# Index scores in blocks of four heads, logits of the first two query blocks for all eight heads, and six softmax steps at new places

## The chip, the cores and the metric

The kernel runs on one core of one Trainium2 chip. The metric is device time in microseconds: the median of three runs for the kernel before, with one profiled execution beside them whose trace is read here.

## The reference

One layer of a decoder trunk, 512 tokens of 1024 channels, batch 1. Cut to what the change touches:

```python
proj = h @ w_in                       # q_att 512, c_kv 128, q_idx 512, k_idx 64, w_idx 8, cv_b/cv_c/cv_x 512 each, two gates 1024 each
raw = einsum('bqhd,bsd->bqhs', q_idx, k_idx) * 64**-0.5       # 8 index heads of 64
score = einsum('bqhs,bqh->bqs', relu(raw), w_idx * 8**-0.5)   # summed over the heads
score = where(causal, score, -inf)
_, sel = top_k(score, 128)                                    # 128 keys for each query
logits = (q_lat . c_sel) * 64**-0.5                           # 8 heads, only the selected keys
probs = softmax(where(valid, logits, -inf));  att = probs @ values
conv_y = cv_b * causal_dwconv(cv_c * cv_x)                    # width 3
merged = sigmoid(g_att) * (att @ w_br_att) + sigmoid(g_conv) * (conv_y @ w_br_conv)
h = layer_norm(ALPHA * h + merged @ w_o);  then a gated MLP with a convolution, and a second layer_norm
```

The first query block of 128 needs no selection (128 keys or fewer are before it), so scores are computed for query blocks 1 to 3 only. "Selected" is turned into a mask: a selected key gets 0, any other a large negative number (`madd`), and the logits are computed for all keys of the causal block and masked.

## The kernel before

All products run on TensorE in split precision: a float32 operand becomes a high part (`wh`, a cast on ScalarE) and a low part (`wl`, the rest, a subtraction on VectorE or on POOL), and `mm3` multiplies high by high, high by low and low by high. A weight chunk of 128 output columns (`fm`) is 8 x 3 = 24 products of 128x128 weights by 512 tokens into one PSUM bank. The weights stream: SP issues the load of a raw chunk (`wr`), `advance` makes its two parts a few steps ahead of use.

The program is written by hand in order: a list of steps, each of which emits its instructions on every engine; each engine runs its own queue in that order. What can wait for what follows from the tiles. `ps` gives PSUM tiles from one rotation of 8 banks; a ninth tile waits until the first of the eight has been read. SBUF tiles of 512 columns (`k2`) rotate over 8 places, larger ones (`k4`) over 28.

The steps around the change, in the order of the program:

- The small projections (key latent, index key, index weights), and the first half (256 tokens) of two convolution chunks, kind c and kind x. Their two PSUM banks (`half_...`, the x chunk's is `half_246`) stay in use until the second halves are done.
- Four index query chunks (`qidx`, j = 0 to 3), each for two heads: 24 products of 384 columns, then a split (`qi0` to `qi3`). After j = 1 the index keys are transposed (`small_keys`, tile `kiT`). 
- Index scores (`scores(b, heads)`): for a query block b and two heads, `mm3_pair` makes 6 products that have only 64 rows, two heads side by side in the two halves of the array, each head in its own bank (`raw`). ScalarE takes the relu into `rl` (8 places), and VectorE adds it, times the head's weight, to the running `score` of that block. The first score block of the program (heads 0, 1 for b = 3, 2, 1) follows j = 2, the second j = 3, the third the second half of the c chunk, the fourth that of the x chunk.
- The second halves: `cvc` copies c to SBUF; `cvx` multiplies x (still in its PSUM bank) by it on VectorE (`cvu`), and `conv_mix` makes three scaled copies on ScalarE (`cvt`, `tap1`, `tap0`), which POOL adds up.
- Then the list `order`: the b chunk of the convolution (the first `cv` product), four attention query chunks (`qatt`), nine convolution chunks (j = 1 to 3), from index 14 on the gates `g` (24 products of 512 columns, 5.4 us) and branch products `r`. After index 8 comes `kproj`, after 10 `vproj`. While these run, VectorE has the selection (`topk`: 16 rounds of `max` and `match_replace` for each of the blocks 1 to 3) beside its ordinary work.
- Attention steps are put ahead of some of these chunks: `ATT_AT` gives their places relative to index 14. Step n makes the logits and the softmax (`att_a`) of one (group of four heads, query block), and transposes the probabilities of step n - 1 (`att_b`); `att_c` at the end of a group multiplies by the values.

A softmax step of four heads: logits on TensorE (`lg`, 12 products of 64 rows), mask and maximum on VectorE, exponentials on ScalarE into `p` with their sums, normalisation on VectorE (L659), and one step later 4 x (b + 1) transposes on TensorE into `pT`.

Of the kernel before, what the change touches and what calls it, by code (L numbers as in the profile page):

```python
# [8 lines left out]
F32 = mybir.dt.float32  # L9
# [4 lines left out]
P = 128  # L14
S = 512
D = 1024
NB = S // P
# [66 lines left out]
class Kern:  # L84
# [2 lines left out]
    LEAD = 3  # L87
    NK4 = 28
    SIDE_NS = 3600
    ATT_AT = (-2, 0, 2, 4, 6, 8, 9, 10, 12, 14)  # L90

    def __init__(self, ctx, tc, a, out):
        self.ctx, self.tc, self.nc, self.a, self.out = ctx, tc, tc.nc, a, out
# [65 lines left out]
    def mm3_pair(self, heads, qs, n):  # L159

        for qp, kp in ((0, 0), (0, 1), (1, 0)):
            for o, q, k, half in heads:
                rows = slice(half * 64, half * 64 + 64)
                self.nc.tensor.matmul(o, q[rows, qp, qs], k[rows, kp, :n], start=qp + kp == 0, stop=qp == 1)
        return [x[0] for x in heads]

    def rstd(self, var):

# [326 lines left out]
    def plan(self):  # L495
        nc, a = self.nc, self.a
# [18 lines left out]

        def wa(i, **kw):
            return chunk(a["w_a"][i], **kw)
# [40 lines left out]
        def scores(b, heads):  # L558
            SB = (b + 1) * P
            if b not in self.score:  # L560
                self.score[b] = self.k4(f"score{b}", F32, (P, SB))
            sc = self.score[b]
            os = self.mm3_pair([(self.ps("raw")[:, :SB], self.qiT[h // 2], self.kiT, h % 2) for h in heads],
                               slice((b - 1) * P, b * P), SB)
            for h, o in zip(heads, os):
                rl = self.k2(f"rl{b}_{h}")[:, :SB]
                nc.scalar.activation(rl, o, AF.Relu, scale=SCALE)
                prev = self.tri[:, S - SB:] if h == 0 else sc
                nc.vector.scalar_tensor_tensor(sc, rl, self.widx[b][:, h:h + 1], prev,
                                               op0=OP.mult, op1=OP.add)  # L570
# [62 lines left out]

        self.attT = []

        def att_a(g, b):
            SB = (b + 1) * P
            qs = slice(b * P, (b + 1) * P)
            mx = self.sm("mx", [P, 4], bufs=2)
            sums = self.sm("sums", [P, 4], bufs=2)  # L640
            pt = [self.k4(f"p{g}_{b}_{i}", F32, (P, 2, S)) for i in range(2)]
            os = []
            for j in (2 * g, 2 * g + 1):
                os += self.mm3_pair([(self.ps("lg")[:, :SB], self.qaT[j], self.kT[j], i) for i in range(2)], qs, SB)
            for i in range(4):
                l = pt[i // 2][:, i % 2, :SB]
                nc.vector.tensor_tensor_reduce(l, os[i], self.madd[b], 1.0, -3.0e38, OP.add, OP.max,
                                               mx[:, i:i + 1])
            nmx = self.sm("nmx", [P, 4], bufs=2)
            nc.vector.tensor_scalar(nmx, mx, -SCALE, None, op0=OP.mult)  # L650
            for i in range(4):
                l = pt[i // 2][:, i % 2, :SB]
                nc.scalar.activation(l, l, AF.Exp, bias=nmx[:, i:i + 1], scale=SCALE,
                                     accum_out=sums[:, i:i + 1])
            rs = self.sm("rs", [P, 4], bufs=2)
            nc.vector.reciprocal(rs, sums)
            for i in range(4):
                l = pt[i // 2][:, i % 2, :SB]
                nc.vector.tensor_scalar(l, l, rs[:, i:i + 1], None, op0=OP.mult)  # L659
            return pt  # L660

        def att_b(g, b, pt):
            pv = self.pv.setdefault(g, {})
            for c in range(b + 1):
                t = self.ps("pT")
                for i in range(4):
                    nc.tensor.transpose(t[:, i * P:(i + 1) * P], pt[i // 2][:, i % 2, c * P:(c + 1) * P],
                                        self.ident)
                if c == b and b % 2:
                    pv[c, b // 2] = self.k2(f"pT{g}_{b}_{c}", F32, (P, 4, P))  # L670
                elif (c, b // 2) not in pv:
                    pv[c, b // 2] = self.k4(f"pT{g}_{b}_{c}", F32, (P, 4, 2 * P))
                at = slice(0, P) if c == b else slice(b % 2 * P, b % 2 * P + P)
                nc.scalar.copy(pv[c, b // 2][:, :, at], t.rearrange("p (h t) -> p h t", h=4))

        def att_c(g):

            for j in range(2 * g, 2 * g + 2):
                o = self.ps("at")
                for half in range(2):  # L680
                    for c in range(2 * half + 2):
                        for i in range(2):
                            x = self.pv[g][c, half][:, 2 * j - 4 * g + i]
                            n = x.shape[-1]
                            h = 2 * j + i
                            nc.tensor.matmul(o[64 * i:64 * i + 64, 256 * half + 256 - n:256 * half + 256],
                                             self.vals[c][:, 64 * h:64 * h + 64], x,
                                             start=c == 0, stop=c == 2 * half + 1, skip_group_check=True)
                t = self.k4(f"at{j}", F32R, (P, 2, S))
                self.evac_split(t[:, 0], t[:, 1], o)  # L690
                self.attT.append(t)
            del self.pv[g]

        self.att_state, self.pv = {}, {}
        seq = [(g, b) for g in range(2) for b in range(NB)]

        def att_step(n):

            def f():
                if n in (5, 9):  # L700
                    att_c(n // 9)
                if 0 <= n - 1 < len(seq):
                    g, b = seq[n - 1]
                    att_b(g, b, self.att_state.pop(n - 1))
                if 0 <= n < len(seq):
                    g, b = seq[n]
                    while b not in self.ready:
                        next(self.side)
                    self.att_state[n] = att_a(g, b)
            return f  # L710


# [103 lines left out]
            return chunk(a["w_b"][i], **kw)  # L816


        def and_scores(j, fn):
            def f():  # L820
                fn()
                if j < 0:
                    self.small_keys()
                    return
                for b in (3, 2, 1):
                    scores(b, range(2 * j, 2 * j + 2))
            return f

        early = [(wa(8 + i, lo="vp"[i], resident=True), kind) for i, kind in enumerate("cx")]
# [1 line left out]
            w.second = in_halves(lambda o, kind=kind: fns[kind](o, 0), w)  # L831
        for j in range(4):
            fn = qidx(j, w := wa(j))
            step(and_scores(j - 2, fn) if j else fn, [w])
        for i, (w, kind) in enumerate(early):
            step(and_scores(2 + i, w.second), [w])
            w.need = 0


# [18 lines left out]
        order = [("b", 0)] + [("q", j) for j in range(4)] + [(kind, j) for j in range(1, 4) for kind in "cxb"]  # L858
        att_at = {len(order) + at: n for n, at in enumerate(self.ATT_AT)}
        order += [("g", 0, 0), ("g", 0, 1), ("g", 1, 0), ("g", 1, 1), ("r", 0, 1),  # L860
# [109 lines left out]
        for kk in range(4):  # L970
            w = wb(kk)
# [42 lines left out]
        pc, w = chunk(a["p_T"]), wb(9)  # L1014
# [292 lines left out]
        for j in range(NF):  # L1307
            if j in BY_BLOCKS:
                for n in range(3):
                    w = chunk(wsum[j][n - 1]) if n else wa(36 + 2 * j)  # L1310
# [5 lines left out]
            for which in (0, 1):  # L1316
                w = wa(36 + 2 * j + which)
# [26 lines left out]
        pairs = BY_BLOCKS[:EARLY], BY_BLOCKS[EARLY:]  # L1344
# [7 lines left out]
        for n, (name, i) in enumerate(copies):  # L1352
            at = at_ple - 2 + n // 2 if n < 4 else at_ple + 1 + (n - 4) * 4 // 5 if n < 20 else at_ple + 16 + 3 * (n - 20)
# [3 lines left out]
        n = len(those)  # L1357
# [317 lines left out]
```

## Time and profile before

| | |
|---|---|
| median of 3 runs | 737.0 us (736.82 to 738.28) |
| profiled execution | 736.87 us, span of the trace 735.1 us, mean granted TensorE clock 0.997 |
| TensorE | 725.5 us busy, 99% of the span, 4255 products |
| VectorE | 590.1 us, 80% |
| ScalarE | 409.9 us, 56% |
| POOL | 243.4 us, 33% |
| chain of work that ended last | TensorE 98%, VectorE 1%, ScalarE 1% |

Shares over the whole span mix stages with different limits. In the rows that follow, a timeline row gives start in us, busy us, engine, line, operation, output and inputs, size, and the number of instructions; what stands in brackets is the idle time ahead of it and what ended it. In a row of the windows view the columns behind the stretch and its length are PE, PEld (weight loads), VectorE, ScalarE, POOL, SP, each with its count, then the granted clock, the DMA share and the GB/s.

### The profile page before, as it was taken

What the parts mean: (1) busy time and instruction counts of PE and PEld (TensorE: products, weight loads), DVE (VectorE), ACT (ScalarE), POOL (GpSimd) and SP (SyncE); (2) the same over time, 40 slices, a digit from 0 to 9 for tenths busy, and PEclk for the clock granted to TensorE, in tenths of its full rate; (3) what the DMA queues carried; (4) which work ended last, traced back from release to release, by engine and by line L of the source; (5) the groups of instructions that cost most, each with busy time, mean ns of one, the idle gap of its engine ahead of it and who ended that gap; (6) DMA issues with size and microseconds to landing.
All of it is one profiled execution on the core that took longest, in us unless ns stands there. A gap on an engine that the chain in (4) does not pass through costs nothing.

```text
span 735.1 us, 11836 instructions
## 1 busy us (share of the span) xinstructions
PE 725.5 (99%) x4255; PEld 633.8 (86%) x4255; DVE 590.1 (80%) x1015; ACT 409.9 (56%) x688; POOL 243.4 (33%) x326
## 2 busy tenths in 40 slices
PE   9999999999999999999999999999999999999996
PEld 5998888888877788888888999999999998888885
DVE  5867999864545266879889899999999889978797
ACT  4647424566656415342675666777767765665640
POOL 4303575555442755010101233343422112311002
PEclk9999999999999999999999999999999999999998
DMA  9372598789997999889767998998899778999761
GB/s 350 109 286 101 159 369 295 238 276 230 190 197 151 230 195 305 302 287 357 299 260 235 301 302 228 251 246 236 247 247 237 223 222 213 277 250 256 256 198 75
DMA packets 61866, 178.00 MB, mean 242 GB/s; under 512 B 7232, under 2 KB 7360, under 8 KB 61424
## 3 DMA queue, kind: packets, MB, share of 16 engines
q1 hardware_dynamic: 43248, 138.43, 53.5%
q0 software_dynamic: 17264, 36.31, 27.6%
q10 hardware_dynamic: 1296, 2.51, 1.0%
q8 instruction: 33, 0.54, 0.3%
q14 instruction: 25, 0.20, 0.1%
HBM read 171.46 MB, written 70.78 MB: 330 GB/s over the span
## 4 chain that ended last, share of the span: by engine, by line
PE 98%; DVE 1%; ACT 1%; issue 0%; DVEq 0%; POOL 0%; POOLq 0%; ACTq 0%
PE ffb L1230 26%; PE dn L1412 5%; PE dn L1413 5%; PE dn L1411 5%; PE gt L155 4%; PE gt L157 4%; PE gt L156 4%; PE cv L155 3%; PE cv L157 2%; PE cv L156 2%; PE wo L812 2%; PE wo L811 2%; PE wo L813 2%; PE br L155 2%; PE br L156 2%; PE br L157 2%
## 5 line engine op out<-in xcount | busy, mean ns | idle before, releaser
L141 DVE TENSOR_TENSOR wl<-wr,wh 128x1024 fp32r<-128x1024 f32 (+1 forms) x171 | 195.4, 1159 | 42.0 <-ACT wh L74 41.1
L74 ACT CAST wh<-wr 128x1024 fp32r<-128x1024 f32 (+1 forms) x182 | 178.1, 986 | 78.1 <-PE dn L1413 11.0
L1338 POOL TENSOR_TENSOR behind<-token,neghalf 128x1 f32<-128x1 f32 x112 | 79.6, 846 | 276.8 <-ACT token L1337 209.7
L1230 PE MATMUL ffb<-hsl,wh 128*128 128x256 f32 x304 | 86.1, 283 | 0.0
L1230 PE MATMUL ffb<-hsh,wl 128*128 128x256 f32 x304 | 86.1, 283 | 0.0
L1230 PE MATMUL ffb<-hsh,wh 128*128 128x256 f32 x304 | 86.1, 283 | 0.0
L1230 PE MATMUL ffb<-h1T,wh 128*128 128x256 f32 x456 | 83.7, 283 | 0.0
L1230 PEld LDWEIGHTS ffb<-h1T,wh 128*128 128x128 f32 x456 | 71.3, 192 | 0.1
L1230 PE MATMUL ffb<-h1T,wl 128*128 128x256 f32 x228 | 64.6, 283 | 0.0
L1230 PEld LDWEIGHTS ffb<-hsh,wh 128*128 128x128 f32 x304 | 58.4, 192 | 0.0
L1230 PEld LDWEIGHTS ffb<-hsl,wh 128*128 128x128 f32 x304 | 58.4, 192 | 0.0
L1230 PEld LDWEIGHTS ffb<-hsh,wl 128*128 128x128 f32 x304 | 58.4, 192 | 0.0
L155 PE MATMUL gt<-hT,wh 128*128 128x512 f32 x128 | 50.5, 394 | 0.0
L156 PE MATMUL gt<-hT,wh 128*128 128x512 f32 x128 | 49.9, 390 | 0.0
L157 PE MATMUL gt<-hT,wl 128*128 128x512 f32 x128 | 49.9, 390 | 0.0
L141 POOL TENSOR_TENSOR wl<-wr,wh 128x1024 fp32r<-128x1024 f32 x15 | 36.2, 2419 | 29.3 <-ACT wh L74 29.3
L1230 PEld LDWEIGHTS ffb<-h1T,wl 128*128 128x128 f32 x228 | 43.8, 192 | 0.0
L173 POOL TENSOR_TENSOR rstd<-veps,neghalf 128x1 f32<-128x1 f32 x12 | 7.1, 591 | 101.4 <-DVE nm L196 67.8
L1203 POOL DMA_DIRECT2D ws<-ws x38 | 36.5, 1333 | 3.6 <-issue 2.2
L1203 POOL DMA_DIRECT2D ws<-in_w_a x38 | 36.0, 1361 | 3.1 <-issue 1.5
L155 PE MATMUL cv<-hT,wh 128*128 128x512 f32 x80 | 31.4, 392 | 0.0
L157 PE MATMUL cv<-hT,wl 128*128 128x512 f32 x80 | 31.2, 390 | 0.0
(336 smaller groups left out, 1929.4 us busy)
## 6 DMA issues: line engine op xcount, KB each, us to landing
wr<-in_w_a SPq DMA_DIRECT2D x61, 512.0 KB, 4.4
ws<-in_w_a SPq DMA_DIRECT2D x76, 256.0 KB, 6.0
wr<-ws SPq DMA_DIRECT2D x38, 512.0 KB, 6.1
ws<-in_w_a POOLq DMA_DIRECT2D x38, 256.0 KB, 8.1
ws<-ws POOLq DMA_DIRECT2D x38, 256.0 KB, 8.3
wr<-in_w_b SPq DMA_DIRECT2D x15, 512.0 KB, 5.6
wr<-in_w_dn SPq DMA_DIRECT2D x15, 512.0 KB, 6.6
wr<-in_w_a SPq DMA_DIRECT2D x19, 256.0 KB, 6.6
```

Source lines behind the costliest of these rows:

```text
L74: nc.scalar.copy(hi, raw)
L141: (self.nc.vector if eng == "v" else self.nc.gpsimd).tensor_tensor(lo, raw, hi.bitcast(F32), op=OP.subtract)
L155: t.matmul(out, wh, xh, start=start, stop=False)
L156: t.matmul(out, wh, xl, start=False, stop=False)
L157: t.matmul(out, wl, xh, start=False, stop=stop)
L811: nc.tensor.matmul(o, act[:, 0, tb], wh, start=start, stop=False, skip_group_check=not check)
L1203: return lambda: nc.gpsimd.dma_start(to, what, accum_op=OP.add, max_dma_last_dim=4096)
L1230: nc.tensor.matmul(o, l[:, c], r, start=start and c + i == 0, stop=stop and c == 3 and i == 2, skip_group_check=True)
L1338: nc.gpsimd.tensor_tensor(self.sm("behind", [P, 1], bufs=2), t, self.neghalf, op=OP.mult)
L1411: nc.tensor.matmul(o, ah, wh[:, i, c], start=first, stop=False, skip_group_check=free)
L1412: nc.tensor.matmul(o, ah, wl[:, i, c], start=False, stop=False, skip_group_check=free)
L1413: nc.tensor.matmul(o, al, wh[:, i, c], start=False, stop=last, skip_group_check=free)
```

## The change

Three things. Scores are made for four heads at a time, so there are two score blocks and not four: heads 0 to 3 behind index query chunk j = 3, heads 4 to 7 behind the second half of the x chunk. A new function, `pair_blocks`, makes each pair of heads by itself and puts as many results into a bank as fit (two of 256 columns, four of 128). The softmax steps of query blocks 0 and 1 take both groups of heads at once, so there are six softmax steps and not eight; their probabilities lie in smaller tiles. And `ATT_AT` has eight places in the place of ten. The new numbers put the steps at indices 12, 14, 16, 19, 21, 23, 26, 28 of `order`; they were at 12, 14, 16, 18, 20, 22, 23, 24, 26, 28.

```diff
-    ATT_AT = (-2, 0, 2, 4, 6, 8, 9, 10, 12, 14)
+    ATT_AT = (-2, 0, 2, 5, 7, 9, 12, 14)
...
+    def pair_blocks(self, nm, pairs, qs, n):
+
+        os, per = [], S // n
+        for i, (q, k) in enumerate(pairs):
+            if i % per == 0:
+                banks = [self.ps(nm) for _ in range(2)]
+            at = slice(i % per * n, i % per * n + n)
+            os += self.mm3_pair([(banks[half][:, at], q, k, half) for half in range(2)], qs, n)
+        return os
...
-            os = self.mm3_pair([(self.ps("raw")[:, :SB], self.qiT[h // 2], self.kiT, h % 2) for h in heads],
-                               slice((b - 1) * P, b * P), SB)
+            os = self.pair_blocks("raw", [(self.qiT[h // 2], self.kiT) for h in heads[::2]],
+                                  slice((b - 1) * P, b * P), SB)
...
-        def att_a(g, b):
+        def att_a(gs, b):
...
-            pt = [self.k4(f"p{g}_{b}_{i}", F32, (P, 2, S)) for i in range(2)]
-            os = []
-            for j in (2 * g, 2 * g + 1):
-                os += self.mm3_pair([(self.ps("lg")[:, :SB], self.qaT[j], self.kT[j], i) for i in range(2)], qs, SB)
+            n = 4 * len(gs)
+            mx, sums, nmx, rs = (self.sm(x, [P, 8], bufs=2)[:, :n] for x in ("mx", "sums", "nmx", "rs"))
+            ls = []
+            for g in gs:
+                if b == 0:
+                    t = self.k2(f"p{g}_{b}", F32, (P, 4, SB))
+                    ls += [t[:, i] for i in range(4)]
+                elif b == 1:
+                    t = self.k4(f"p{g}_{b}", F32, (P, 4, SB))
+                    ls += [t[:, i] for i in range(4)]
+                else:
+                    t = [self.k4(f"p{g}_{b}_{i}", F32, (P, 2, S)) for i in range(2)]
+                    ls += [t[i // 2][:, i % 2, :SB] for i in range(4)]
+            os = self.pair_blocks("lg", [(self.qaT[2 * g + i], self.kT[2 * g + i]) for g in gs for i in range(2)],
+                                  slice(b * P, (b + 1) * P), SB)
...
-        seq = [(g, b) for g in range(2) for b in range(NB)]
+        seq = [((0, 1), 0), ((0, 1), 1), ((0,), 2), ((0,), 3), ((1,), 2), ((1,), 3)]
...
-                if n in (5, 9):
-                    att_c(n // 9)
+                if n in (5, 7):
+                    att_c(n // 7)
                 if 0 <= n - 1 < len(seq):
-                    g, b = seq[n - 1]
-                    att_b(g, b, self.att_state.pop(n - 1))
+                    gs, b = seq[n - 1]
+                    ls = self.att_state.pop(n - 1)
+                    for i, g in enumerate(gs):
+                        att_b(g, b, ls[4 * i:4 * i + 4])
...
-                for b in (3, 2, 1):
-                    scores(b, range(2 * j, 2 * j + 2))
+                for b in (3, 2, 1):
+                    scores(b, range(2 * j, 2 * j + 4))
...
-            step(and_scores(j - 2, fn) if j else fn, [w])
+            step(fn if j in (0, 2) else and_keys(fn) if j == 1 else and_scores(0, fn), [w])
         for i, (w, kind) in enumerate(early):
-            step(and_scores(2 + i, w.second), [w])
+            step(and_scores(2, w.second) if i else w.second, [w])
```

The rest of `att_a` is as before, with loops over 4 or 8 heads. The order of instructions moves at three places that matter below.

TensorE, the score block behind the second half of the x chunk. `raw` is a bank with scores, `qi2` and `qi3` the index queries of heads 4, 5 and 6, 7; "waits" names the engine whose work must be done first. Before, its first and last rows and the b chunk behind it:

```order
L164 MATMUL raw_289_952<-kiT_669,qi3_788 128x512 [waits Activation_49]
L164 MATMUL raw_290_953<-kiT_669,qi3_788 128x512 [waits Activation_49]
...
L164 MATMUL raw_293_980<-kiT_669,qi3_788 128x256 [waits Activation_49]
L164 MATMUL raw_294_981<-kiT_669,qi3_788 128x256 [waits Activation_49]
...
L155 MATMUL cv_299_1018<-hT0_178,wh17_757 128x512 [waits Activation_49]
```

And after:

```order
L164 MATMUL raw_281_908<-kiT_669,qi2_709 128x512 [waits Activation_49]
...
L164 MATMUL raw_287_944<-kiT_669,qi3_743 128x384 [waits Activation_49]
L164 MATMUL raw_288_945<-kiT_669,qi3_743 128x384 [waits DVE_49]
...
L164 MATMUL raw_289_964<-kiT_669,qi2_709 128x256 [waits Activation_49]
L164 MATMUL raw_290_965<-kiT_669,qi2_709 128x256 [waits Activation_49]
...
L164 MATMUL raw_290_965<-kiT_669,qi3_743 128x256
L155 MATMUL cv_295_1014<-hT0_178,wh17_712 128x512 [waits Activation_49]
```

Six banks became ten (raw_281 to raw_290); the eighth, raw_288, waits for VectorE, the ninth and tenth for ScalarE.

VectorE, from the last score updates ahead of `cvu0` (the product that reads the x chunk's bank) on. `rl1_4` is the relu of query block 1, head 4. Before:

```order
L569 SCALAR_TENSOR_TENSOR score1_742<-rl1_4_901,widx_204_195,score1_742 128x256
L569 SCALAR_TENSOR_TENSOR score1_742<-rl1_5_904,widx_204_195,score1_742 128x256
L141 TENSOR_TENSOR wl19_908<-wr19_585,wh19_907 128x1024
L743 TENSOR_TENSOR cvu0_942<-half_246_449,cvc0_863 128x512
L569 SCALAR_TENSOR_TENSOR score3_712<-rl3_6_960,widx_206_197,score3_712 128x512
```

And after:

```order
L579 SCALAR_TENSOR_TENSOR score1_804<-rl1_2_825,widx_204_195,score1_804 128x256
L579 SCALAR_TENSOR_TENSOR score1_804<-rl1_3_828,widx_204_195,score1_804 128x256
L141 TENSOR_TENSOR wl19_864<-wr19_585,wh19_863 128x1024
L757 TENSOR_TENSOR cvu0_898<-half_246_449,cvc0_861 128x512
L579 SCALAR_TENSOR_TENSOR score3_746<-rl3_4_924,widx_206_197,score3_746 128x512
```

Before, the updates of six heads stood ahead of `cvu0` and those of two behind; now it is four and four, and all of the four ahead come from the one block behind j = 3.

ScalarE, the exponentials of the second group (`p1_...`) and the casts between them, one cast (`wh`) to a chunk of products. Before:

```order
L653 ACTIVATE p1_1_1_2467,sums_486_2465<-p1_1_1_2467,nmx_491_2488 128x256 x2
L74 CAST wh42_2500<-wr42_2168 128x1024
...
L653 ACTIVATE p1_2_1_2565,sums_503_2563<-p1_2_1_2565,nmx_508_2586 128x384 x2
L74 CAST wh43_2598<-wr43_2202 128x1024
L674 COPY pT1_2_0_2657<-pT_520_2652 128x4x128
```

And after:

```order
L668 ACTIVATE p1_2_1_2405,sums_463_2401<-p1_2_1_2405,nmx_464_2402 128x384 x2
L74 CAST wh41_2436<-wr41_2103 128x1024
L74 CAST wh42_2467<-wr42_2153 128x1024
...
L686 COPY pT1_2_0_2573<-pT_488_2568 128x4x128
```

Between the exponentials of a step and the copies of its transposed probabilities there was one chunk's cast; now there are two.

More of the change, by code (lines that the diff above doesn't have):

```diff
@@ L634, in plan @@
         self.attT = []
-        def att_a(g, b):
+        def att_a(gs, b):
             SB = (b + 1) * P
-            qs = slice(b * P, (b + 1) * P)
-            mx = self.sm("mx", [P, 4], bufs=2)
-            sums = self.sm("sums", [P, 4], bufs=2)
-            pt = [self.k4(f"p{g}_{b}_{i}", F32, (P, 2, S)) for i in range(2)]
-            os = []
-            for j in (2 * g, 2 * g + 1):
-                os += self.mm3_pair([(self.ps("lg")[:, :SB], self.qaT[j], self.kT[j], i) for i in range(2)], qs, SB)
-            for i in range(4):
-                l = pt[i // 2][:, i % 2, :SB]
+            n = 4 * len(gs)
[13 more added lines that the diff above has]
+                                  slice(b * P, (b + 1) * P), SB)
+            for i, l in enumerate(ls):
@@ L647, in att_a @@
                 nc.vector.tensor_tensor_reduce(l, os[i], self.madd[b], 1.0, -3.0e38, OP.add, OP.max,
                                                mx[:, i:i + 1])
-            nmx = self.sm("nmx", [P, 4], bufs=2)
             nc.vector.tensor_scalar(nmx, mx, -SCALE, None, op0=OP.mult)
-            for i in range(4):
-                l = pt[i // 2][:, i % 2, :SB]
+            for i, l in enumerate(ls):
                 nc.scalar.activation(l, l, AF.Exp, bias=nmx[:, i:i + 1], scale=SCALE,
                                      accum_out=sums[:, i:i + 1])
-            rs = self.sm("rs", [P, 4], bufs=2)
@@ L656, in att_a, with att_b @@
             nc.vector.reciprocal(rs, sums)
-            for i in range(4):
-                l = pt[i // 2][:, i % 2, :SB]
+            for i, l in enumerate(ls):
                 nc.vector.tensor_scalar(l, l, rs[:, i:i + 1], None, op0=OP.mult)
-            return pt
-        def att_b(g, b, pt):
+            return ls
+        def att_b(g, b, ls):
             pv = self.pv.setdefault(g, {})
@@ L666, in att_b @@
                 for i in range(4):
-                    nc.tensor.transpose(t[:, i * P:(i + 1) * P], pt[i // 2][:, i % 2, c * P:(c + 1) * P],
-                                        self.ident)
+                    nc.tensor.transpose(t[:, i * P:(i + 1) * P], ls[i][:, c * P:(c + 1) * P], self.ident)
                 if c == b and b % 2:
@@ L694, in plan @@
         self.att_state, self.pv = {}, {}
-        seq = [(g, b) for g in range(2) for b in range(NB)]
+        seq = [((0, 1), 0), ((0, 1), 1), ((0,), 2), ((0,), 3), ((1,), 2), ((1,), 3)]
         def att_step(n):
             def f():
-                if n in (5, 9):
-                    att_c(n // 9)
+                if n in (5, 7):
+                    att_c(n // 7)
                 if 0 <= n - 1 < len(seq):
-                    g, b = seq[n - 1]
-                    att_b(g, b, self.att_state.pop(n - 1))
+                    gs, b = seq[n - 1]
+                    ls = self.att_state.pop(n - 1)
+                    for i, g in enumerate(gs):
+                        att_b(g, b, ls[4 * i:4 * i + 4])
                 if 0 <= n < len(seq):
-                    g, b = seq[n]
+                    gs, b = seq[n]
                     while b not in self.ready:
                         next(self.side)
-                    self.att_state[n] = att_a(g, b)
+                    self.att_state[n] = att_a(gs, b)
             return f
@@ L816, in wb, with and_keys, f @@
             return chunk(a["w_b"][i], **kw)
+        def and_keys(fn):
+            def f():
+                fn()
+                self.small_keys()
+            return f
         def and_scores(j, fn):
@@ L821, in f @@
                 fn()
-                if j < 0:
-                    self.small_keys()
-                    return
                 for b in (3, 2, 1):
-                    scores(b, range(2 * j, 2 * j + 2))
+                    scores(b, range(2 * j, 2 * j + 4))
             return f
```

## The prediction

> **What bounds the kernel.** I read the page's span and chain, then the stages, then TensorE's waits, then the timelines of each engine where the diff works.
>
> ```profile
> span 735.1 us, 11836 instructions
> PE 98%; DVE 1%; ACT 1%; issue 0%; DVEq 0%; POOL 0%; POOLq 0%; ACTq 0%
> 67.10:137.60 70.50, 70.50 (x311) 58.40 (x312) 64.53 (x149) 31.76 (x50) 46.33 (x27) 1.00 0.72 244
> PE pT L667 <- DVE p L659: 0.6, 1, 0.6
> ```
>
> TensorE carries 98% of the chain, so a change is worth what it moves on TensorE's queue. VectorE is close behind in the stage after the index scores: 64.53 of 70.50 us. Whatever makes TensorE wait for VectorE's queue there is paid in full.
>
> **Part 1, fewer switches to 64-row products.** One such block in the old order, with its neighbours:
>
> ```profile
> 60.07 0.28 PE L156 MATMUL half<-hT,wh 128*128 128x256 f32 x1
> 60.19 0.28 PE L157 MATMUL half<-hT,wl 128*128 128x256 f32 x1
> 60.40 1.84 PE L164 MATMUL raw<-kiT,qi 64*128 64x512 f32 x18
> 62.17 0.39 PE L155 MATMUL half<-hT,wh 128*128 128x256 f32 x1
> 62.39 0.28 PE L156 MATMUL half<-hT,wh 128*128 128x256 f32 x1
> ```
>
> The half chunk's products follow each other every 0.12 us. Into the block it is 0.21 (0.09 more); the block takes 1.77 to the next product where its nine pairs at 0.23, 0.17 and 0.12 us (the spacing of products of 512, 384 and 256 columns) make 1.55 (0.22 more); the product behind it takes 0.22 (0.10 more). A switch in and out costs 0.41 us. Four score blocks become two (-0.8), eight logit blocks six (-0.8 by the same price).
>
> **Part 2, ten banks wanted by one score block, eight there.** The first new block stands right behind the fourth index query chunk.
>
> ```profile
> 49.17 1.85 PE L164 MATMUL raw<-kiT,qi 64*128 64x512 f32 x18
> 51.19 0.44 PE L155 MATMUL qi<-hT,wh 128*128 128x384 f32 x1 [0.16 <-ACT rl L567]
> 55.55 1.85 PE L164 MATMUL raw<-kiT,qi 64*128 64x512 f32 x18
> 50.54 1.09 ACT L567 ACTIVATE rl<-raw 128x512 f32<-128x512 f32 x2 [0.78 <-PE raw L164]
> 56.55 0.60 ACT L567 ACTIVATE rl<-raw 128x512 f32<-128x512 f32 x1 [0.41 <-PE raw L164]
> ```
>
> Without the block at 49.17 that chunk starts at 49.17 - 0.09 = 49.08 instead of 51.19, and its first product is not slow (0.1), so the block starts 2.2 us before 55.55, at 53.3. The old order already once waited for a relu (0.16). Relus of 512 columns come every 0.49 us, the first 1.0 us after the block's start: the fourth ends at 53.3 + 1.0 + 3 x 0.49 + 0.6 = 56.4. The built program lets the tenth bank wait for that one. Unhindered TensorE would be there at 53.3 + 2.5 = 55.8, so it stalls 0.6, and the c chunk's second half starts at 57.3, about when it did (57.34). The x chunk's follows with no block between; its 48 products end the stretch at 63.0, and the second block starts at 63.2, 2.0 us before the old fourth one.
>
> There the eighth bank (raw_288) is the one in which the x chunk was summed. It is free when VectorE has run cvu0, the product that reads it; the ninth and tenth wait for the block's first two relus, and ScalarE has those behind cvt and two taps, which also wait for cvu0. Queued ahead of cvu0 on VectorE are the first block's twelve score updates and wl19:
>
> ```profile
> 51.17 0.75 DVE L569 SCALAR_TENSOR_TENSOR score<-rl,widx,tri 128x512 f32<-128x512 f32 x1 [0.82 <-ACT rl L567]
> 52.02 0.75 DVE L569 SCALAR_TENSOR_TENSOR score<-rl,widx,score 128x512 f32<-128x512 f32 x1
> 59.96 2.67 DVE L569 SCALAR_TENSOR_TENSOR score<-rl,widx,score 128x256 f32<-128x256 f32 x1
> 63.14 3.84 DVE L569 SCALAR_TENSOR_TENSOR score<-rl,widx,score 128x512 f32<-128x512 f32 x6
> 66.89 1.22 DVE L141 TENSOR_TENSOR wl<-wr,wh 128x1024 fp32r<-128x1024 f32 x1
> 68.03 0.68 DVE L743 TENSOR_TENSOR cvu<-half,cvc 128x512 f32<-128x512 f32 x1
> 59.96 2.39 POOL L141 TENSOR_TENSOR wl<-wr,wh 128x1024 fp32r<-128x1024 f32 x1 [19.99 <-ACT wh L74]
> 67.58 1.68 POOL L607 TENSOR_TENSOR w_uk<-w_uk_raw,w_uk 128x512 fp32r<-128x512 f32 x1 [5.23 <-ACT w_uk L606]
> ```
>
> Updates begin 0.63 after the first relu's start (51.17 behind 50.54): 53.3 + 1.0 + 0.63 = 54.95. Six take 3.84; twelve take 7.7, and 0.4 more since four in a row on one score each wait 0.1 for the last write (51.17 + 0.75 to 52.02): 63.05. The update at 59.96 took 2.67 instead of some 0.5: POOL's wl18 began with it, and it ended 0.28 behind POOL. In the new order ScalarE's cast for wl18 again follows the relus, again near 58.8, so an update that begins at about 60.3 is held to 62.35 + 0.4: 1.9 more, 64.95. Then wl19 (1.22) and cvu0 from 66.0.
>
> One more POOL product can stand in the way, w_uk's low half:
>
> ```profile
> 63.25 0.34 ACTq L604 DMA_DIRECT2D w_uk_raw<-in_w_uk  x1
> 66.89 0.62 ACT L606 CAST w_uk<-w_uk_raw 128x512 fp32r<-128x512 f32 x1 [2.16 <-DMA w_uk_raw<-in_w_uk]
> 68.81 0.82 ACT L729 ACTIVATE cvt<-cvu,vec 128x512 f32<-128x512 f32 x1 [1.30 <-DVE cvu L743]
> 70.76 1.05 ACT L567 ACTIVATE rl<-raw 128x512 f32<-128x512 f32 x2
> 67.02 0.50 PE L155 MATMUL cv<-hT,wh 128*128 128x512 f32 x1
> DMA to landing us min/median/max: 2.8/2.8/2.8
> ```
>
> Its load is issued once ScalarE's queue has passed the c half's wait, near 60.5, and lands 3.6 us later (63.25 to 66.89) or 2.8 (its sister load w_uv_raw, the last line); with the cast POOL starts between 64.0 and 64.8 and runs 1.68, just where the last updates and wl19 stand. Held, VectorE loses 0.9 to 1.5. I take 1.2: the window covers wl19's start in most of its width. cvu0 then starts at 67.2. From there: in the old order the second relu behind cvu0 ended at 70.76 + 1.05 = 71.81, 3.78 after cvu0's start; then three pairs of 256 columns for the second half of that bank and three before them (0.6 to the last), 0.2 out of the block. So the b chunk (cv, 67.02 before) starts 4.6 us after cvu0, at 71.8: +4.8 for the scores, the two saved switches already in it. Bounds: cvu0 at 66.0 gives +3.6; both POOL products out of the way +1.8; no bank wait at all -1.0 (0.8 and the old 0.2 wait). Topk begins some 2 to 4 us later, TensorE more than that, so VectorE's backlog gets no nearer.
>
> **Part 3, the spacing.** In the old order the last softmax steps stood one product apart:
>
> ```profile
> 190.81 0.60 PE L667 MATMUL pT<-ident,p 128*128 128x128 f32 x4
> 191.34 0.89 PE L164 MATMUL lg<-kT,qa 64*128 64x128 f32 x12
> 214.94 1.46 PE L667 MATMUL pT<-ident,p 128*128 128x128 f32 x8
> 216.33 1.34 PE L164 MATMUL lg<-kT,qa 64*128 64x384 f32 x12
> 222.95 0.39 PE L157 MATMUL br<-cvT,wl 128*128 128x512 f32 x1
> 223.98 2.19 PE L667 MATMUL pT<-ident,p 128*128 128x128 f32 x12 [0.64 <-DVE p L659]
> 226.10 1.65 PE L164 MATMUL lg<-kT,qa 64*128 64x512 f32 x12
> ```
>
> Four undisturbed transposes take 0.53 with the switch behind them, 0.11 each. Eight should take 0.97 and took 1.39; twelve should take 1.4 and took 2.12, and stood 0.8 late (222.95 to 223.98, where 0.23 is due). With 0.1 ahead of the eight that is 2.0 us of waiting for p. Now two or three products (5.4 us each) stand between, against one. All of it goes: -2.0. With two logit blocks less -2.8.
>
> What may be late next is p of the eight-head steps.
>
> ```profile
> 156.98 1.14 DVE L659 TENSOR_SCALAR p<-p,rs 128x256 f32<-128x256 f32 x4
> 162.24 0.93 PE L667 MATMUL pT<-ident,p 128*128 128x128 f32 x7
> ```
>
> Four heads of block 1 were ready at 158.1, 4.1 us before their transposes. Eight heads cost some 1.4 (maxima), 2.0 (exponentials) and 1.1 (this row) more, 4.5, and block 0's 3.2 more stand ahead in the same queue; against it TensorE comes 4.8 (scores) and 1.8 (its own added logits and transposes) later there, less VectorE's 2 to 3.5 in the backlog. That nets to a slack of 0 to 2 us: 0.1 for the forecast, up to 1 at the upper end. Fewer small operations and the halved k4 use change nothing on TensorE's queue: VectorE works beside it.
>
> **Sum.** +4.8 - 2.8 + 0.1 = +2.1, and I shade it to +1.9 because a stall's end can fall with work already queued. The profiled execution took 736.87, 0.1 under the runs' median of 737.0, so 738.8 us. The before runs spread 736.82 to 738.28: 0.2% (1.5 us) is what a measurement can tell.
>
> **Rivals.** (a) POOL's w_uk product misses VectorE's two-input work: +3.6 - 2.8, 737.6. For it: at 66.89 wl19 was already running and was not held. (b) The change does what it says: banks are free in time, -1.0 - 2.8, 733.1. It needs cvu0 done at 65.0 and two relus by 65.6, where even the unhindered queue puts cvu0 past 64; against it stands that order. (c) In between, no POOL hold at all: +1.8 - 2.8, 735.9. The decisive point for "faster" is cvu0 starting before 65. (d) The clock falls. TensorE would stand still from 65.2 to 67.9, 2.7 us at a stretch.
>
> ```profile
> 726.00:728.00 2.00, 1.92 (x16) 1.71 (x15) 0.91 (x3) 0.34 (x1) 1.58 (x1) 1.00 0.09 34
> 730.00:732.00 2.00, 0.00 (x0) 0.00 (x0) 2.00 (x4) 0.00 (x0) 0.40 (x1) 0.74 0.35 131
> ```
>
> At the end of the run products stop at 727.9, and a clock of 0.74 over 730 to 732, 0.50 after it, puts the fall at 731.0, 3.0 us of idleness later. The new stall comes within 0.3 of that. At half clock the rest of the block and the b chunk (6 us) would take up to 6 more; I set 3: 741.8. [...]
>
> **Chances.** Forecast 0.52 (own range 737.7 to 740.2); (a) 0.17; (b) 0.10; (c) 0.08; (d) or a late p of about that size 0.13. Leaving out (b) and the upper half of (d) gives 735.4 to 741.0. Slower by over 0.2% (above 738.5): six tenths of the forecast's share and all of (d), 0.45. Faster (below 735.5): (b) and half of (c), 0.15. Same: 0.40.
>
> **What would show it.** A second score block (raw, 36 products) that starts near 63 and stretches to some 8 us with TensorE waiting for cvu and then for rl; the b chunk's first product near 72; the first block 0.6 stretched; an update of over 2 us beside wl18; wl19 or an update held beside w_uk; transposes at the old 215 and 224 without waits; a clock of 1.00 throughout. The prediction is wrong if the second block takes under 4 us, or if new waits for p appear at the transposes of block 1.

## The result and the profile after

The changed kernel takes 742.79 us (median of 6 runs, 742.26 to 744.38) against 737.57 us before (6 runs, 736.62 to 738.49): a ratio of 1.0074, interval 1.0060 to 1.0088, so 5.2 us slower. The forecast was 738.8 us with a range up to 741.0.

The page, the chain of waits of TensorE and its timeline around the second score block. Rows of the page are busy time, share and instructions; a row of waits is total, times, longest in us:

```profile
span 741.4 us, 11838 instructions
PE 728.2 (98%) x4255; PEld 636.1 (86%) x4255; DVE 592.8 (80%) x1011; ACT 410.6 (55%) x688; POOL 242.4 (33%) x326
...
PE raw L164 <- DVE cvu L757: 2.3, 1, 2.3
PE raw L164 <- ACT rl L577: 1.8, 1, 1.8
...
63.74 2.35 PE L164 MATMUL raw<-kiT,qi 64*128 64x512 f32 x19
68.36 0.79 PE L164 MATMUL raw<-kiT,qi 64*128 64x384 f32 x5 [2.27 <-DVE cvu L757]
70.97 2.13 PE L164 MATMUL raw<-kiT,qi 64*128 64x256 f32 x12 [1.81 <-ACT rl L577]
73.02 0.79 PE L155 MATMUL cv<-hT,wh 128*128 128x512 f32 x1
...
77.88 0.46 PE L157 MATMUL cv<-hT,wl 128*128 128x512 f32 x1
78.18 0.40 PE L155 MATMUL cv<-hT,wh 128*128 128x512 f32 x1
```

TensorE stands twice in the second block, 2.27 us for `cvu` and 1.81 us for the relus, where the block before never waited. Behind it the b chunk's products come every 0.43 us up to 77.88, and every 0.23 us only from 78.18 on. In the windows view the products' busy time (the first figure behind the length of the stretch) and the granted clock (the third from the end) show why:

```profile
64.36:67.77 3.41, 1.73 (x17) 1.24 (x13) 3.20 (x5) 0.00 (x0) 1.29 (x1) 1.00 0.32 126
67.77:71.19 3.42, 1.02 (x6) 0.66 (x6) 0.78 (x2) 2.79 (x5) 1.26 (x1) 1.00 0.44 153
71.19:74.60 3.41, 3.33 (x16) 2.64 (x16) 3.10 (x4) 3.35 (x9) 1.42 (x1) 0.50 0.00 0
74.60:78.02 3.42, 3.42 (x10) 2.65 (x9) 3.11 (x5) 1.70 (x3) 1.14 (x1) 0.50 0.00 0
78.02:81.43 3.41, 3.41 (x17) 2.78 (x16) 3.10 (x5) 0.00 (x0) 1.25 (x1) 1.00 0.29 79
```

The clock falls at 71.19 and is back at 78.02, 6.83 us later. The b chunk starts at 73.02 and not 67.02. The profiled execution had been 0.39 us later than the one before already ahead of the index queries (36.05 and not 35.66), so 5.6 us of that belong to the change. The b chunk itself takes 7.92 us (73.02 to 80.94), not 5.59.

The queues ahead of the first wait, on VectorE and POOL:

```profile
60.80 2.58 DVE L579 SCALAR_TENSOR_TENSOR score<-rl,widx,score 128x384 f32<-128x384 f32 x1
...
64.48 1.50 DVE L579 SCALAR_TENSOR_TENSOR score<-rl,widx,score 128x256 f32<-128x256 f32 x1
...
66.48 1.22 DVE L141 TENSOR_TENSOR wl<-wr,wh 128x1024 fp32r<-128x1024 f32 x1
67.62 0.68 DVE L757 TENSOR_TENSOR cvu<-half,cvc 128x512 f32<-128x512 f32 x1
...
60.48 2.48 POOL L141 TENSOR_TENSOR wl<-wr,wh 128x1024 fp32r<-128x1024 f32 x1 [20.13 <-ACT wh L74]
64.41 1.29 POOL L617 TENSOR_TENSOR w_uk<-w_uk_raw,w_uk 128x512 fp32r<-128x512 f32 x1 [1.44 <-DVE score L579]
```

One update of 384 columns took 2.58 us beside POOL's wl18, where the two ahead of it took 0.62 each: 2.0 us held. One of 256 columns took 1.50 beside w_uk, where the one ahead of it and the one behind took 0.49 and 0.48: 1.0 us held. `cvu` starts at 67.62.

In the softmax steps the old waits for p are gone, and one row is longer than its like before:

```profile
172.44 1.91 PE L680 MATMUL pT<-ident,p 128*128 128x128 f32 x16
174.27 2.04 PE L164 MATMUL lg<-kT,qa 64*128 64x384 f32 x12
176.25 0.50 PE L155 MATMUL gt<-hT,wh 128*128 128x512 f32 x1
...
225.39 1.53 PE L680 MATMUL pT<-ident,p 128*128 128x128 f32 x12
...
  ACT sig L795: 0.6, 2
```

Twelve transposes take 1.53 where they took 2.19 before. The logits at 174.27 take 1.98 us to the next product, where the same block took 1.27 before (216.33 to 217.60); the last row, from the view of the logits' tile, says what ended that idleness: a sigmoid, which reads the bank that the logits want. (ScalarE loads a table for 1.28 us just ahead of the two sigmoids, from 172.91 on.) From the first logit to the first branch product behind the last value product TensorE needs 115.84 us (146.31 to 262.15) against 117.93 (137.98 to 255.91).

So the trace has +4.9 us of waits in the score blocks, +3.0 of half clock and -2.1 in the softmax steps, 5.8 together; the medians differ by 5.2, the two spans by 6.3 (741.4 less 735.1).

### The profile page after: what moved, and what is told of

It is laid out like the page before. It is cut to its first block, busy times and chain, and to the rows that moved or that the text cites. A ratio compares the mean times of both kernels' runs of the same rounds, so it can differ in the third digit from the quotient of the medians.

```text
span 741.4 us, 11838 instructions
## 1 busy us (share of the span) xinstructions
PE 728.2 (98%) x4255; PEld 636.1 (86%) x4255; DVE 592.8 (80%) x1011; ACT 410.6 (55%) x688; POOL 242.4 (33%) x326
## 4 chain that ended last, share of the span: by engine, by line
PE 90%; DVE 6%; ACT 2%; DMA 2%; issue 1%; DVEq 0%; ACTq 0%
PE ffb L1247 26%; PE dn L1428 5%; PE dn L1430 5%; PE dn L1429 5%; PE gt L155 4%; PE gt L157 3%; PE gt L156 3%; PE br L155 2%; PE wo L827 2%; PE wo L826 2%; PE br L157 2%; PE br L156 2%; PE wo L825 2%; PE cv L155 2%; PE cv L156 2%; PE cv L157 2%
## 5 line engine op out<-in xcount | busy, mean ns | idle before, releaser
L1355 POOL TENSOR_TENSOR behind<-token,neghalf 128x1 f32<-128x1 f32 x112 | 75.7, 765 | 266.4 <-ACT token L1354 207.7
L1220 POOL DMA_DIRECT2D ws<-ws x38 | 34.0, 1101 | 8.6 <-issue 5.2
L155 PE MATMUL cv<-hT,wh 128*128 128x512 f32 x80 | 32.4, 405 | 0.0
L156 PE MATMUL cv<-hT,wh 128*128 128x512 f32 x80 | 32.1, 401 | 0.0
```

Of the source, the lines that this page charges most:

```text
L155: t.matmul(out, wh, xh, start=start, stop=False)
L156: t.matmul(out, wh, xl, start=False, stop=False)
L1220: return lambda: nc.gpsimd.dma_start(to, what, accum_op=OP.add, max_dma_last_dim=4096)
L1355: nc.gpsimd.tensor_tensor(self.sm("behind", [P, 1], bufs=2), t, self.neghalf, op=OP.mult)
```

## The experiments

The forecast had the waits; it had the clock at 1.00. The theory after the result: the two waits together let the clock fall, and score part and softmax part add up. Each of the first four experiments changes one thing. The code shows the lines that matter; the comments in it are the document's.

**One part at a time.** The first has the new softmax steps with the old score blocks, the second the new score blocks with the old softmax steps:

```diff
-        step(fn if j in (0, 2) else and_keys(fn) if j == 1 else and_scores(0, fn), [w])
+        step(and_scores(j - 2, fn) if j else fn, [w])           # and two heads in scores()
```

> The new softmax steps with the old four score blocks of two heads. Theory (the loss is in the second score block, the gain in the softmax steps, and the two add up): the trace of the changed kernel took 115.8 us from the first logit to the last value product against 117.9 before, so 2.1 us faster than before, 735.4 us against 737.5, no wait for cvu in the score blocks, clock 0.997. Rival (the softmax part gains only because TensorE came 8 us late and everything else was ready): within 0.5 us of before.

Measured: 736.79 us against 736.96, ratio 1.0000 (0.9992 to 1.0009). The theory's 2.1 us did not come; the rival has it. From the waits and the timeline of this run:

```profile
PE pT L680 <- DVE p L672: 1.3, 1, 1.3
...
165.69 2.51 PE L680 MATMUL pT<-ident,p 128*128 128x128 f32 x16 [1.28 <-DVE p L672]
168.13 2.08 PE L164 MATMUL lg<-kT,qa 64*128 64x384 f32 x12
```

Without the 8 us of lateness, the eight-head step of query block 1 has its p too late: TensorE waits 1.3 us, its sixteen transposes take 0.6 more than above, and the logits wait for the sigmoid as in the changed kernel.

> The old softmax steps with the new score blocks of four heads. Theory: +4.9 us for the waits for banks and +3.0 us for about 6.8 us at half clock behind them, so 7.9 us slower than before, 745.4 us, mean clock 0.992. Rival (the later start of TensorE takes away the old waits for p in the softmax steps, so the parts do not add up): 743.5 us.

Measured: 744.43 us, ratio 1.0098 (1.0085 to 1.0111), so 7.2 us slower, nearer the theory's 7.9 than the rival's 6.0 (743.5 less 737.5). The waits and the half clock (70.45 to 77.27, 6.83 us) are those of the changed kernel, and the old softmax steps take 117.97 us from 145.91, as they did from 137.98. The old steps take the same time at both starts; the new ones do not.

**Work in place of the waits.** The two waits are filled with products that nobody reads:

```diff
+            if i == len(pairs) - 1:
+                for bank, cnt in zip(banks, fill):      # fill = (20, 16) for heads 4-7, b = 2
+                    for _ in range(cnt):
+                        self.nc.tensor.transpose(bank[:, :P], self.ident, self.ident)
```

> The changed kernel with 20 extra transposes of the identity on TensorE ahead of the wait for cvu and 16 behind it, ahead of the wait for the relu; their results are written over. They take 2.2 and 1.8 us, about the two waits, so nothing else comes later. Theory (idleness in those 5 us lets the clock fall): the clock stays at 1.00, the b chunk has its products 0.23 us apart from the start, and the time falls by the 3.0 us of the half clock, to 739.8 us. Rival (the clock falls for another reason, the 64-row products or a fixed moment): the clock falls again near 71 us and the time stays at 742.8 us or above.

Measured: 740.75 us, ratio 1.0049 (1.0037 to 1.0061). Timeline of TensorE:

```profile
65.37 4.45 PE L177 MATMUL raw<-ident 128*128 128x128 f32 x36
69.75 2.17 PE L164 MATMUL raw<-kiT,qi 64*128 64x384 f32 x18
71.85 0.50 PE L155 MATMUL cv<-hT,wh 128*128 128x512 f32 x1
72.19 0.40 PE L156 MATMUL cv<-hT,wh 128*128 128x512 f32 x1
```

The clock stays at 1.00, and the b chunk runs at full pace from its start. The attention queries behind it start at 77.42 against 80.94; with the 0.46 by which this execution was earlier at the index queries (35.59 against 36.05) that is 3.06 us, the price of the half clock. In the time some 1.8 of them are seen (the ratios 1.0074 and 1.0049 are 0.25% apart): the softmax steps behind take 116.81 us and not 115.84.

**One wait less.** The scaled copies for the convolution go behind the first four relus on ScalarE's queue:

```diff
                 for b in (3, 2, 1):
                     scores(b, range(2 * j, 2 * j + 4))
+                    if j and b == 3:
+                        self.late_mix()                 # cvt, tap1, tap0: were emitted in cvx
```

> The changed kernel with the scaled copies cvt and tap on ScalarE behind the first four relus of the second score block, not ahead of them. The ninth and tenth bank then need not wait for cvu; the wait of the eighth bank (2.4 us) stays. Theory A (the clock fell because of both waits together, some 4.4 us idle of 5.2): the clock stays at 1.00, the b chunk starts 3.3 us earlier than in the changed kernel, near 69.7 us, and the time is 737.2 us. Theory B (the first wait of 2.4 us alone is enough, the fall comes some 5 us behind its start whatever follows): the clock falls near 71 us all the same, about 3.4 us are lost behind it, 740.6 us.

Measured: 738.42 us, ratio 1.0026 (1.0016 to 1.0036). Timeline, and the two windows with the stand:

```profile
67.90 1.50 PE L164 MATMUL raw<-kiT,qi 64*128 64x384 f32 x17 [2.30 <-DVE cvu L757]
69.33 0.50 PE L155 MATMUL cv<-hT,wh 128*128 128x512 f32 x1
...
63.62:67.03 3.41, 1.97 (x19) 1.44 (x15) 3.20 (x4) 2.31 (x5) 1.29 (x1) 1.00 0.35 141
67.03:70.45 3.42, 2.55 (x22) 2.24 (x23) 3.21 (x5) 2.51 (x5) 1.01 (x1) 1.00 0.46 153
```

In this execution it went as theory A says: the second wait is gone, the first is still there, and the clock stays. (A later execution of the same kernel went otherwise; see below.) The b chunk starts at 69.33. Against before it is 1.9 us slower by the ratio, where theory A had 0.3 faster; 1.6 of that are the softmax steps, 117.43 us with a wait of 0.8 for p. One of the twelve executions took 742.45 at a clock of 0.993.

**What lets the clock fall.** Two runs put ten stands of TensorE into the kernel before. Each stand takes a bank from the rotation; these two runs are read for the clock alone:

```diff
+                nc.tensor.transpose(o[:, :P], self.ident, self.ident)
+                nc.scalar.copy(s[0], o[:, :P])
+                for k in range(STANDS[i] - 1):
+                    nc.scalar.copy(s[(k + 1) % 2], s[k % 2])
+                nc.tensor.transpose(o[:, P:2 * P], s[(STANDS[i] - 1) % 2], self.ident)
```

> The kernel before with ten stands put into TensorE's queue ahead of chunks 2, 5, 8, 11, 13, 17, 20, 25, 29 and 33 of the list: one transpose, then 3 to 8 copies of 128x128 one behind the other on ScalarE, then a transpose that waits for the last. TensorE should stand 1.5 to 3.5 us at each (longer where ScalarE has other work queued). Theory W (the clock is set from the share of work in stretches of some 3.4 us that run on by themselves; the half clock of the changed kernel lasted 6.84 us, two of them): stands under 2 us never let it fall, those of 2.4 to 3.4 sometimes, longer ones nearly always, and all moments of change lie on one grid of about 3.42 us. Theory L (a count from the last product, 3.0 us as at the end of the run): every stand over 3.0 us lets it fall just 3.0 us behind its start, none below does, and there is no grid.

> The same with other numbers of copies at the ten places (5 to 9). Theory W: again one grid of 3.42 us, and at a given length a fall at some places and none at others. Theory L: a fall at each stand over 3.0 us, 3.0 us behind its start.

Measured: 799.05 and 806.67 us, one run each, with eight and nine falls ahead of the one at the end. The stands came out at 1.7 to 10.4 us. All changes of the clock in each of these traces lie on one grid: half-clock stretches last 3.41, 6.83 or 10.24 us, full ones (in the first run) 3.41 times 4, 5, 7, 8 or 29, and in the trace of after the one from 78.02 to 736.79 us is 193 times 3.413. Stretches of that grid, three of the first run and three of the second:

```profile
104.55:107.96 3.41, 1.29 (x7) 0.78 (x5) 3.24 (x9) 2.14 (x4) 1.58 (x2) 1.00 0.90 298
107.96:111.38 3.42, 2.33 (x6) 1.94 (x7) 0.29 (x1) 0.94 (x4) 2.61 (x2) 0.50 0.85 273
...
278.63:282.04 3.41, 1.65 (x8) 1.39 (x9) 2.32 (x9) 3.22 (x8) 0.68 (x2) 1.00 0.87 196
...
212.20:215.62 3.42, 1.73 (x8) 1.46 (x9) 1.91 (x9) 3.26 (x8) 1.09 (x4) 1.00 1.12 235
...
232.69:236.10 3.41, 1.14 (x6) 0.66 (x4) 0.46 (x8) 2.04 (x7) 2.61 (x8) 1.00 0.75 238
236.10:239.52 3.42, 3.36 (x16) 3.36 (x17) 0.00 (x0) 1.47 (x4) 3.42 (x9) 0.50 0.91 149
```

A stretch with 1.29 or 1.14 us of products is followed by half clock, one with 1.65 or 1.73 is not (the full clock goes on at 215.62 and at 282.04). Over ten traces (those of before and after and eight of the runs) all 29 full-clock stretches with at most 0.38 of their time in products, by the durations of their rows, were followed by a fall, and none of those with 0.48 or more; none lay between. The three traces of the last round add four falls, two of them behind stretches with 0.42 and 0.43. The runs agree with theory W and not with theory L: of two stands of 2.3 us in the second run one (233.83 to 236.16) let the clock fall and one (211.62 to 213.90) did not, and a stand of 3.2 us (277.18 to 280.39 in the first run) did nothing: the grid cuts it into parts of 1.45 and 1.76 us, and the two stretches had 1.96 and 1.65 us of products, 0.57 and 0.48 of their time.

With the two waits 4.1 us of idleness lie in 4.9, and some stretch of 3.41 holds at least 2.04 of them wherever the grid lies, so that at most 0.40 of it are products. All ten executions with both waits (six of the changed kernel, four of the second experiment) have a mean granted clock of 0.992 to 0.994, where the kernel before has 0.995 to 0.999.

**How often one stand does it.** The relus-first kernel again:

> The relus-first kernel once more, for how often one stand of 2.3 us lets the clock fall. In the traces a stretch of 3.413 us with at most 0.38 of its time in products was followed by half clock, one with 0.48 or more was not. A stand of 2.3 us puts more than 2.1 us of idleness into one such stretch in (3.41 - 2.30 + 2 x 0.18) / 3.41 = 43% of the positions. Theory (positions are even): four to six of about twelve executions near 741.5 us, the others near 738.4. Rival (the stretches stand in a nearly fixed relation to the start of the program): nearly all at 738.4 again, as eleven of twelve before.

Measured: 738.63 us, ratio 1.0020 (1.0006 to 1.0035); nine of twelve within 738.26 to 738.91, the others 739.05, 739.81 and 740.97. By these times the theory of even positions would be refuted, for four to six were expected near 741.5. But the times can't count the falls. The profiled execution is the fastest of the twelve, 738.26 us, and in it the one stand let the clock fall:

```profile
65.89:69.30 3.41, 1.46 (x18) 1.32 (x18) 3.31 (x5) 1.76 (x4) 0.00 (x0) 1.00 0.29 96
69.30:72.72 3.42, 3.42 (x9) 2.74 (x9) 3.21 (x4) 1.87 (x5) 2.70 (x2) 0.50 0.14 58
...
67.84 1.50 PE L164 MATMUL raw<-kiT,qi 64*128 64x384 f32 x17 [2.33 <-DVE cvu L757]
69.27 0.79 PE L155 MATMUL cv<-hT,wh 128*128 128x512 f32 x1
```

Here most of the stand lies in one stretch of the grid, which has 0.43 of its time in products; in the execution shown above the grid cut it at 67.03, and the two stretches had 0.58 and 0.75. So one stand is enough at some positions of the grid and not at others, and neither theory A nor theory B of that experiment holds as it was put. The fall shows in no time because the loss of 1.5 us ahead of the softmax steps (first logit at 141.83, not 140.28) is gone behind them: VectorE began the p of query block 1 at the same time in both (166.85 and 166.86), so the wait of 0.8 for p is not there, the transposes take 0.6 less, and the branch products start at 257.75 and 257.71. A long execution is no sign of a fall either: the kernel before had three of 740.5 to 741.1 us in the same round. How often one stand does it stays open; of two traces one shows it. The rival, a nearly fixed relation to the start of the program, does not hold: in the thirteen traces the first line of the grid lies anywhere from 0.16 to 2.92 us behind the first instruction (0.53 before, 2.92 after, 2.18 and 1.04 in the two executions of this kernel).

**Towards a better kernel.** The third softmax step one chunk later, with the old score blocks:

```diff
-    ATT_AT = (-2, 0, 2, 5, 7, 9, 12, 14)
+    ATT_AT = (-2, 0, 3, 5, 7, 9, 12, 14)
```

> The old score blocks of two heads with the new softmax steps, and the third softmax step one chunk later (index 17 of the list, not 16), so that the transposes of the eight-head step for query block 1 stand behind three chunks and not two. Theory (the new softmax steps gave nothing with the old scores because TensorE waited 1.3 us for p ahead of those transposes, 0.7 between them, and 0.7 in the logits behind them for the sigmoids): these 2.6 us go, 734.2 us against 736.9 before. Rival (p waits for VectorE's selection of block 3, and whatever stands a chunk later there waits elsewhere): 736.5 us, with a new wait at the next step.

Measured: 734.32 us (733.98 to 734.5), ratio 0.9963 (0.9950 to 0.9975), the fastest of all. Timeline of TensorE at the moved step:

```profile
169.96 1.91 PE L680 MATMUL pT<-ident,p 128*128 128x128 f32 x16
171.80 1.33 PE L164 MATMUL lg<-kT,qa 64*128 64x384 f32 x12
173.06 0.50 PE L155 MATMUL gt<-hT,wh 128*128 128x512 f32 x1
```

No wait for p, and logits in 1.26 us: the sigmoids are done at 169.7. The softmax steps take 115.33 us (138.14 to 253.47), 2.8 less than the same steps at index 16.

The four-head blocks without their waits: relus first, and the four updates of query block 1 behind `cvu`:

```diff
+                if b == 1 and h < 4:
+                    self.late_sums.append(add)          # emitted behind cvu
+                else:
+                    add()
```

> The changed kernel with relus ahead of cvt and tap as in the last run, with the four score updates of query block 1 of the first score block put behind cvu on VectorE, not ahead of it, and with the third softmax step at index 17. Theory: cvu starts near 64.6 us and frees its bank ahead of the eighth bank's product at 65.5, no wait over 0.3 us in the second block, the b chunk near 66.6 us (66.9 before), clock 1.00 throughout; with the softmax steps as in the run beside it 733.8 us. Rival (wl19 and POOL's w_uk product still keep cvu until 66.4): the b chunk near 68 us and 735.3 us.

Measured: 735.26 us, ratio 0.9976 (0.9966 to 0.9986). The score part is the theory's, the time nearer the rival's:

```profile
64.12 0.68 DVE L766 TENSOR_TENSOR cvu<-half,cvc 128x512 f32<-128x512 f32 x1
...
63.41 3.43 PE L164 MATMUL raw<-kiT,qi 64*128 64x512 f32 x36
66.77 0.50 PE L155 MATMUL cv<-hT,wh 128*128 128x512 f32 x1
...
152.02 0.82 PE L689 MATMUL pT<-ident,p 128*128 128x128 f32 x4 [1.20 <-DVE p L681]
...
148.68 3.78 DVE L681 TENSOR_SCALAR p<-p,rs 128x128 f32<-128x128 f32 x8
149.42 2.36 POOL L141 TENSOR_TENSOR wl<-wr,wh 128x1024 fp32r<-128x1024 f32 x1 [9.16 <-ACT wh L74]
```

`cvu` runs at 64.12, TensorE no longer waits, and the b chunk starts at 66.77, 0.4 earlier than in the run beside it (67.17). But now the first eight-head p is late by 1.2 us. The eight normalisations take 3.78 us because one of them stands beside POOL's `wl`, but so they do in the run beside it (3.81), where p is late by 0.25 at most (its eight transposes take 1.28 us, where they take 1.03 after the change). What differs is that VectorE begins the eight 0.9 later (148.68, not 147.74) and TensorE comes 0.4 earlier. The merged score blocks, even without their waits, give no gain over the old ones (735.26 and 734.32 us).

> The four-head score blocks without their waits (relus ahead of cvt, cvu ahead of the last four updates) with the second and third softmax step at indices 15 and 17. In the run before, the transposes of the eight-head step of query block 0 waited 1.2 us for p and took 0.4 longer after it. Theory (VectorE's p is late by that much and no more): the 1.6 us go, 733.7 us, and no wait of TensorE over 0.3 us between 60 and 250 us. Rival (VectorE is so close behind that the wait moves to the next step): 735 us with a wait for p at the transposes near 165 us.

> The two-head score blocks with the same places of the softmax steps, 15 and 17. Theory: the transposes behind the first step took 1.21 us where 0.96 is due, so 0.2 us less than with 14 and 17, 734.1 us; the four-head blocks of the run beside it are worth 0.4 us against it (b chunk at 66.6 and not 67.0). Rival (the second step's logits a chunk later make its p late for the transposes at 17): 735.5 us.

Measured: 736.35 us (ratio 0.9990, 0.9971 to 1.0010) and 735.21 us (0.9974, 0.9960 to 0.9988): 0.9 to 1.1 us more than with the second step at index 14, with intervals that overlap; the traces have a new wait. The rivals were nearer, though what waits is not p:

```profile
173.33 0.79 PE L164 MATMUL lg<-kT,qa 64*128 64x384 f32 x5 [0.83 <-ACT pT L686]
```

With the second step a chunk later too, the logits at index 17 find their banks still held by ScalarE's copies of the transposed p (row of the two-head run; the other has the same wait of 0.8, and 0.8 for a gate's bank besides).

## Why the prediction was wrong

- **The waits for banks were right.** The step "+4.8 for the scores" came out at 4.9: the b chunk 5.6 late, less 0.7 of half clock in the block's own end (the six pairs from 71.45 took 1.57 us, and 0.90 in the first block). Its parts hold too. `cvu` was set at 67.2 (by the working's own terms 67.3: 64.95 and wl19's 1.14 are 66.1, not 66.0) and started at 67.62 less 0.39. wl18's hold was 1.9 in the working and 2.0 in the trace, w_uk's 1.2 and 1.0. The first block's stall was 0.6 and measured 0.7 (4.07 us to the next product, where the 36 products of the second block took 3.36 without waits, in the run with `cvu` early). Rivals (a), (b) and (c) all needed less of it, and none came.
- **The step that failed is the clock.** The sum of the forecast has no term for it. The text set the new stall against the 3.0 us of idleness ahead of the fall at the run's end and wrote "comes within 0.3 of that", for a single stand of 2.7 us, and gave it a part of 0.13, together with a late p. It was two stands, 2.27 and 1.81, neither near 3.0, with 0.8 of work between, and the clock fell for 6.83 us. What went with a fall in these traces was not a stand's length but the share of products in a stretch of the 3.41 us grid: at most 0.43, and 0.30 here (1.02 of 3.42 us). Two gaps of 2.3 and 1.8 us were enough, in two traces a single one of 2.3, and one of 3.2 us was not. The forecast's own second wait, for the relus behind `cvu`, was left out of rival (d); with both, that share would have made the fall all but certain. The price of 3 us for the case was measured at 3.06, but it was set at half of "up to 6" without a reason, so the near hit of 741.8 is luck. The direction was right. The range was cut through the middle of that case.
- **The spacing was right in its mechanism, but a new wait was put at almost nothing.** The old waits for p went: -2.0 in the forecast, -2.06 in the traces (from the product ahead to the one behind, the steps at 214.94 and 223.98 took 3.02 and 4.73 us, their undisturbed likes at 162.24 and 175.50 took 2.47 and 3.22). Against them stands the wait of 0.7 for the sigmoids, which the text put at 0.1 together with all other new waits. In sum the steps gained 2.1, so the two logit blocks less were worth some 0.7, where the forecast had 0.8.
- **The slack of "0 to 2 us" for the eight-head p was real** and the two parts of the change leaned on it: with TensorE not late, 1.3 us of waiting for p came, and the softmax part alone gave nothing. From the first logit to the branch products the new steps took 118.14, 117.43, 116.81 and 115.84 us where TensorE began at 137.91, 140.28, 142.80 and 146.31. From run to run, each microsecond saved ahead of them was paid back by 0.25 to 0.3, until the step was moved. In the repeat of the relus-first kernel, where the half clock alone made TensorE late (141.83, then 115.92 us), the whole 1.5 us came back.

## What to carry to other kernels

The longest wait did not tell whether the clock would fall here (2.3 us was enough, 3.2 us was not); the share of products in a stretch of 3.41 us did (a fall at 0.43 or less, none at 0.48 or more). Look for a fall in the trace, not in the time: the 1.5 us that one cost here vanished in a later wait. Two waits of 2 us a microsecond apart cost 4 us of standing here and 3 more of half clock, and where they can't be taken away, work that nobody reads in their place gives back the 3 at that place (1.8 in the time). Before two blocks are merged into one, count the banks that the larger one wants at once, and see what stands ahead of the readers that free them on their own queues. A gain in a late stage that rests on TensorE coming late is not a gain: measure each part alone, and space the steps for the kernel that will be kept.

## What the runs showed of the hardware

The clock's grid of 3.413 us (658.77 us in 193 stretches after the change), with a fall behind every full-clock stretch that had at most 0.43 of its time in products, and none behind 0.48 or more, in thirteen traces, was not expected. Nor was that an operation of VectorE with a single tensor input is held beside POOL's `wl`. By form, the normalisations of after with 128 and with 256 columns:

```profile
L672 DVE TENSOR_SCALAR p<-p,rs 128x128 f32<-128x128 f32 x8 | 3.8, 548 | 0.0
L672 DVE TENSOR_SCALAR p<-p,rs 128x256 f32<-128x256 f32 x8 | 2.2, 351 | 0.0
```

The narrower ones take longer, 548 ns in the mean against 351. Seven of the eight took 0.27 to 0.29 us; the fifth, which began 0.04 us behind `wl` (154.31 to 156.70), took 2.43 and ended 0.08 behind it. The fifth is held in all nine traces of kernels with the eight-head steps (the eight took 3.80 us here and 3.81, 3.78 and 3.82 in three of the others); before, the eight of that width took 283 ns in the mean.
